# A hybrid encoder step on one core: the small group of the w_down product goes last, and the last pair of w_up runs its seven products in another order

## The chip, the cores and the metric

The kernel runs on one core of one Trainium2 chip. The metric is the device time of one execution in microseconds (us). Five engines work side by side: PE (TensorE, matrix products; PEld is its weight load), DVE (VectorE), ACT (ScalarE), POOL (GpSimd) and SP (SyncE, which here only issues transfers, in order, each after the waits that stand on it).

## The reference

One layer of a streaming encoder, for 512 prompt tokens and 128 sample tokens (640 in all), model width 2048. The part that the change touches is the channel mixer at the end:

```python
h = rmsnorm(x, g_pre_mlp) * (1 + scale_m) + shift_m
f = jnp.square(jax.nn.relu(h @ w_up)) @ w_down      # w_up 2048 x 8192, w_down 8192 x 2048
return x + gate_m * rmsnorm(f, g_post_mlp)
```

Before it stand the modulation, the input projection, two attentions, a linear recurrence and the output projection. All data is float32.

## The kernel before

**Products.** Every float32 operand is split into a rounded part and a rest (`split_into`, lines 85 and 86: a cast on ACT, a subtraction on DVE), and each product is three matmuls: high by high, high by rest, rest by high. Large products are taken as 2 x 2 blocks with seven block products in place of eight, after Strassen: sums and differences of blocks are formed on DVE, split, and multiplied; the results are added with signs.

**w_up.** The 8192 columns are 64 tiles of 128, taken in pairs j = 0 to 31. Three pairs are done plainly; pairs 3 to 31 are made by `up_pair(j)`, a generator with a `yield` after most of its products, so that the tail of one pair is interleaved with the head of the next. Its products run in the order 1, 2, 5, 6, 3, 7, 4, each 24 matmuls of 320 columns. Products 1, 2, 4 and 5 read the activations from the buffers `AH` and `AL` (mix_hi and mix_lo); products 3, 6 and 7 read sums of them from six tiles named X. Squared results go to DRAM in 16 blocks `u_dr[0]` to `u_dr[15]`; pair j writes into `u_dr[j // 2]`, so the last pair writes into `u_dr[15]`.

**w_down.** The stage after it adds up, into the tile `acc` (640 tokens by 2048 columns), the products of the blocks u_dr with w_down. Blocks 0 to 14 go through `groups`: a big group takes two blocks, cut into two halves h; the one small group takes a single block, its two halves being the two sides of the 2 x 2 scheme, so that it has half as many matmuls. The small group is block 0 and stands first; then come seven big groups, blocks 1 to 14. Block 15 is done plainly at the end (`down_cols`).

Each group has two passes over the columns, `columns(g, 0, ...)` and `columns(g, 1, ...)`, each with the products 1, 2, 5, 6, 3, 7, 4. In the first and second and in the third and seventh, the sample tokens ride along in a bank named y. A product needs its weights (`w_half`: w11 comes into the pool `wl`, the others w21, w12, w22 and v21 into a ring of six tiles named raw), the weights' sums (line 1173), their split, and its activations, which `u_operands(g)` loads from u_dr, combines and splits into `AX_h` and `AX_l` (ud_hi, ud_lo in the trace): a11, a12, a22 less a21, and so on, and the sample's s0, s1 and their difference. There is one set of these; `columns(g, 1, building)` makes the set of the next group place by place, as soon as a product has read the old one. For group 0 the whole generator is run ahead of the first pass. `gather` adds a bank into `acc` (lines 1123 to 1127).

AX_h and AX_l lie where mix_hi and mix_lo lay (tags `AH`, `AL`), and everything in the pool `ph3` (acc, `at`, `ar`, `wl`) lies where the X tiles and the tiles of w_up's results lay. Before the change a new pool waits for all that lay in its memory.

**Order.** A scheduler puts each engine's instructions in one fixed order; the order of the program and `tc.high_priority` steer it. SP issues nearly all transfers and waits at each.

Of the kernel before, what the change touches and what calls it, by code (L numbers as in the profile page):

```python
# [39 lines left out]
def stream_step(ctx: ExitStack, tc: tile.TileContext, I, O):  # L40
# [951 lines left out]
    with tc.tile_pool(name="up", bufs=1) as pl:  # L992
        def piece(name):
            return pl.tile([P, H2], F32, tag="c", bufs=7, name=name)

        def up_pair(j):

            w = up_blocks(j, "11 21 12 22")
            b1 = bank("mm", f"u1_{j}")
            up_product(1, b1, w["11"], f"a{j}", True)  # L1000
            c = piece(f"c11_{j}")
            S.copy(c, b1[:, :H2])
            yield
# [12 lines left out]
            with tc.high_priority(200):  # L1016
                V.tensor_add(w["11"], w["11"], w["22"])
            up_product(6, b1, w["11"], f"d{j}", False)
            c = piece(f"c12_{j}")
            S.copy(c, b1[:, :H2])  # L1020
            yield
            up_product(3, b2, w["22"], f"e{j}", False)
            V.tensor_add(c, b2[:, :H2], c)
            up_out(c, 2 * j + 1, 0, ALU.min)
            yield
            with tc.high_priority(200):
                V.tensor_add(w["12"], w["12"], w["22"])
            up_product(7, b1, w["12"], f"f{j}", False)
            V.tensor_add(p5, b1[:, :H2], p5)  # L1029
            up_out(p5, 2 * j + 1, 1, ALU.min)  # L1030
            yield
            with tc.high_priority(200):
                V.tensor_add(w["11"], w["11"], w["21"])
            up_product(4, b1, w["11"], f"g{j}", False)
            c = piece(f"c21_{j}")
            S.activation(c, b1[:, :H2], AF.Relu)
            S.activation(c, c, AF.Square)
            nc.sync.dma_start(u_dr[j // 2][:, 2 * j % 4, H2:], c)


        before = None
        for j in range(NPLAIN, 32):
            pair = up_pair(j)
            for i in range(5):
                next(pair)
                if before and i < 2:
                    next(before, None)
            before = pair
        for _ in before:
            pass  # L1050
# [4 lines left out]

    with tc.tile_pool(name="ph3", bufs=1) as pl:
        acc = pl.tile([P, NT, D], F32, name="acc")
        NBLK = 16  # L1060
        ORDER = (1, 2, 5, 6, 3, 7, 4)
        AX_h = act.tile([P, 8704], F32R, tag="AH", name="ud_hi")
        AX_l = act.tile([P, 8704], F32R, tag="AL", name="ud_lo")

        groups = [[((0, 0), (0, 1))]] + [[((n, h), (n + 1, h)) for h in range(2)] for n in range(1, NBLK - 1, 2)]

        def place(i, h):

# [3 lines left out]

        def u_part(g, r, t0, w, tag, name):

            x = pl.tile([P, len(groups[g]), 2, w], F32, tag=tag, bufs=1 if tag == "at" else 2, name=name)
            if len(groups[g]) == 2:
                nc.sync.dma_start(x.rearrange("p h k q -> p (h k) q"), u_dr[groups[g][0][r][0]][:, :, t0 : t0 + w])
            else:
                n, h = groups[g][0][r]
                nc.sync.dma_start(x[:, 0], u_dr[n][:, 2 * h : 2 * h + 2, t0 : t0 + w])  # L1080
            return x.rearrange("p h k q -> p (h k q)")

        def u_split(g, i, x):
            c = slice(place(i, 0).start, place(i, 0).start + x.shape[-1])
            split_into(AX_h[:, c], AX_l[:, c], x)

        def u_operands(g):

            one = lambda r, t, name: u_part(g, r, 256 * t, 256, "ar", f"{name}_{g}")
            u_split(g, 1, one(0, 0, "a11"))  # L1090
            yield
            u_split(g, 2, one(1, 0, "a12"))
            yield
# [11 lines left out]
            a = one(0, 0, "c11")  # L1105
            V.tensor_sub(a, a, one(0, 1, "c21"))
            u_split(g, 7, a)
            x1, x2 = [u_part(g, r, TP, TS, "ar", f"s{r}_{g}") for r in range(2)]
            u_split(g, -1, x1)
            u_split(g, -2, x2)  # L1110
            V.tensor_sub(x2, x2, x1)
            u_split(g, -3, x2)
            yield
            u_split(g, 4, one(1, 1, "b22"))
            yield
# [14 lines left out]
        def w_half(g, h, r, cb, tag, name):  # L1130

            n, q = groups[g][h][r]
            src = I["w_down"][n, cb][:, 1024 * q : 1024 * q + 1024]
            with tc.high_priority(200):
                if tag == "raw":
                    return load(src, f"{name}_{g}{cb}{h}")
                w = pl.tile([P, 1024], F32, tag=tag, bufs=4, name=f"{name}_{g}{cb}{h}")
                nc.sync.dma_start(w, src)
                return w
# [22 lines left out]
                        xs = [x[:, at + P * kk : at + P * kk + P] for x in (AX_h, AX_l)]  # L1162
                        dot(ps, xs, hi, lo, kk, s_first and h == 0 and kk == 0, s_last and h == nh - 1 and kk == 1)

        def columns(g, cb, building):

            nm, hs = f"d{g}{cb}", range(len(groups[g]))
            done = lambda: next(building, None)

            def more(a, b):  # L1170
# [6 lines left out]
            y1 = bank("md", f"{nm}y1")  # L1177
            w11 = [w_half(g, h, 0, cb, "wl", "w11") for h in hs]
            w21 = [w_half(g, h, 1, cb, "raw", "w21") for h in hs]
            product(g, 1, w11, b1, True, nm, (-1, y1, True, False))  # L1180
            for p in range(2):
                gather(p, cb, b1[p], 1)
            done()
            w12 = [w_half(g, h, 0, cb + 2, "raw", "w12") for h in hs]
            w22 = [w_half(g, h, 1, cb + 2, "raw", "w22") for h in hs]
            product(g, 2, w21, b3, True, nm, (-2, y1, False, True))
            for p in range(2):
                gather(p, cb, b3[p], 1)
# [1 line left out]
            done()  # L1190
            b2 = [bank("s", f"{nm}2{p}") for p in range(2)]
            more(w11, w12)
            product(g, 5, w11, b2, True, nm)
            for p in range(2):
                gather(2 + p, cb + 2, b2[p], -1)
            done()
            more(w11, w22)
            product(g, 6, w11, b1, False, nm)
            for p in range(2):
                gather(p, cb + 2, b1[p], -1)  # L1200
            done()
            y2 = bank("md", f"{nm}y2")
            product(g, 3, w22, b2, False, nm, (-3, y2, True, False))
            for p in range(2):
                gather(p, cb + 2, b2[p], -1)
            done()
            more(w12, w22)
            w21 = [w_half(g, h, 1, cb, "raw", "v21") for h in hs]
            product(g, 7, w12, b1, False, nm, (-1, y2, False, True))
            for p in range(2):  # L1210
                gather(2 + p, cb + 2, b1[p], -1)
            gather(4, cb + 2, y2, 1)
            done()
            more(w11, w21)
            product(g, 4, w11, b1, False, nm)
            for p in range(2):
                gather(2 + p, cb, b1[p], 1)
            done()

        for _ in u_operands(0):  # L1220
            pass
        for g in range(len(groups)):
            columns(g, 0, iter(()))
            columns(g, 1, u_operands(g + 1) if g + 1 < len(groups) else iter(()))


        n = NBLK - 1
# [168 lines left out]
```

## Time and profile before

| | us |
|---|---|
| three runs | 2752.97, 2754.78, 2750.55; median 2752.97 |
| the profiled execution | 2754.47 |
| its span | 2752.4 |
| PE busy in the span | 2651.9 (96%) |
| DVE busy | 1749.0 (64%) |
| ACT busy | 1075.0 (39%) |

The profiled execution's own time is 2.1 us above its span and 1.5 us above the median of the runs. PE is the engine that is nearly always busy; where it isn't, the profile says what it waited for.

### The profile page before, as it was taken

The numbers are of one execution on the slowest core, as the hardware profiler recorded it, in microseconds if no ns is written. First come the engines' busy times: TensorE is split into PE (matmuls) and PEld (weight loads), VectorE is DVE, ScalarE is ACT, GpSimd is POOL, SyncE is SP. The second block draws the span as 40 slices with busy tenths as digits, with TensorE's granted clock in tenths as the row PEclk, the third lists the DMA queues.
The fourth block names the chain that finished last, engine by engine and source line by source line (L and its number), as shares of the span: only waits on it lengthen the run. The fifth ranks groups of instructions, "written<-read, shape, count | busy, mean of one in ns | idle before, by whom it ended". The sixth has DMA issues, their size and how long they took to land.

```text
span 2752.4 us, 39345 instructions
## 1 busy us (share of the span) xinstructions
PE 2651.9 (96%) x15574; PEld 2271.7 (83%) x15574; DVE 1749.0 (64%) x2604; ACT 1075.0 (39%) x1641; POOL 53.2 (2%) x103
## 2 busy tenths in 40 slices
PE   7999999999999998999999999997799999999998
PEld 4677788778768777899999999996588887787886
DVE  4465534344354256766666666665888988888977
ACT  4264433334343256533333333332333433333432
POOL 0000000000000001100000000000000000000000
PEclk9999999999999999999999999999899999999999
DMA  8954565666665467733333333334444554554434
GB/s 324 358 161 149 154 193 173 218 209 193 217 218 168 138 218 262 241 114 119 105 118 111 111 118 107 116 113 148 148 155 152 161 173 141 158 179 131 155 106 171
DMA packets 189671, 461.29 MB, mean 168 GB/s; under 512 B 22920, under 2 KB 94248, under 8 KB 186928
## 3 DMA queue, kind: packets, MB, share of 16 engines
q1 hardware_dynamic: 185216, 441.68, 48.9%
q0 software_dynamic: 4128, 17.04, 1.7%
q8 instruction: 122, 2.00, 0.3%
q14 instruction: 61, 0.50, 0.1%
q10 hardware_dynamic: 144, 0.07, 0.0%
HBM read 411.33 MB, written 47.40 MB: 167 GB/s over the span
## 4 chain that ended last, share of the span: by engine, by line
PE 80%; DVE 10%; DMA 6%; issue 2%; ACT 2%; SPq 0%; POOL 0%; DVEq 0%; ACTq 0%; POOLq 0%
PE u L895 9%; PE u L896 9%; PE u L897 9%; PE d L1143 4%; PE d L1144 4%; PE d L1145 4%; PE wo L757 3%; PE wo L758 2%; PE wo L759 2%; DVE d_l L86 2%; DVE ud_lo L86 2%; DMA c<-u_dr 2%; PE mm_ps L142 2%; DVE acc L1123 1%; DMA u<-in_w_up_dram 1%
## 5 line engine op out<-in xcount | busy, mean ns | idle before, releaser
L85 ACT CAST d_h<-w 128x1024 fp32r<-128x1024 f32 x210 | 220.7, 1052 | 404.3 <-PE d L1145 112.8
L1143 PE MATMUL d<-d_h,ud_hi 128*128 128x512 f32 x840 | 330.8, 394 | 23.7 <-ACT ud_hi L85 10.2
L1144 PE MATMUL d<-d_l,ud_hi 128*128 128x512 f32 x840 | 330.0, 393 | 2.8 <-DVE d_l L86 2.8
L1145 PE MATMUL d<-d_h,ud_lo 128*128 128x512 f32 x840 | 328.6, 392 | 1.8 <-DVE ud_lo L86 1.8
L86 DVE TENSOR_TENSOR d_l<-w,d_h 128x1024 fp32r<-128x1024 f32 x210 | 255.5, 1222 | 92.3 <-ACT d_h L85 79.3
L1143 PEld LDWEIGHTS d<-d_h,ud_hi 128*128 128x128 f32 x840 | 158.7, 189 | 62.5 <-DVE acc L1123 14.1
L1144 PEld LDWEIGHTS d<-d_l,ud_hi 128*128 128x128 f32 x840 | 159.1, 189 | 36.9 <-DVE d_l L86 4.2
L1145 PEld LDWEIGHTS d<-d_h,ud_lo 128*128 128x128 f32 x840 | 159.1, 189 | 36.5 <-DVE ud_lo L86 3.5
L1123 DVE TENSOR_TENSOR acc<-acc,d 128x512 f32<-128x512 f32 x208 | 137.4, 682 | 7.7 <-PE d L1145 7.7
L758 PE MATMUL wo<-wo_l,mix_hi 128*128 128x512 f32 x320 | 125.8, 393 | 1.4 <-DVE wo_l L86 1.4
L757 PE MATMUL wo<-wo_h,mix_hi 128*128 128x512 f32 x320 | 126.5, 396 | 0.0
L759 PE MATMUL wo<-wo_h,mix_lo 128*128 128x512 f32 x320 | 125.5, 393 | 0.0
L86 DVE TENSOR_TENSOR wo_l<-wo_r,wo_h 128x1024 fp32r<-128x1024 f32 x48 | 58.6, 1224 | 101.4 <-ACT wo_h L85 98.6
L1173 DVE TENSOR_TENSOR w<-w,w 128x1024 f32<-128x1024 f32 x90 | 109.3, 1221 | 0.7
L86 DVE TENSOR_TENSOR a_l<-u,a_h 128x1024 fp32r<-128x1024 f32 x41 | 50.2, 1225 | 71.2 <-ACT a_h L85 71.2
L85 ACT CAST wo_h<-wo_r 128x1024 fp32r<-128x1024 f32 x48 | 50.1, 1050 | 108.9 <-PE wo L759 96.8
L86 DVE TENSOR_TENSOR g_l<-u,g_h 128x1024 fp32r<-128x1024 f32 x29 | 35.5, 1225 | 64.6 <-ACT g_h L85 64.6
L757 PEld LDWEIGHTS wo<-wo_h,mix_hi 128*128 128x128 f32 x320 | 60.5, 189 | 16.3 <-issue 3.5
L211 PE MATMUL zg<-h_hi,zg_h 128*128 128x320 f32 x224 | 74.0, 330 | 0.0
L211 PE MATMUL zx<-h_hi,zx_h 128*128 128x320 f32 x224 | 73.7, 329 | 0.0
L85 ACT CAST b_h<-u 128x1024 fp32r<-128x1024 f32 x41 | 43.0, 1048 | 75.5 <-PE u L896 60.1
L895 PE MATMUL u<-mix_hi,g_h 128*128 128x320 f32 x232 | 71.8, 310 | 0.6 <-DVE p L1029 0.6
(1867 smaller groups left out, 7390.3 us busy)
## 6 DMA issues: line engine op xcount, KB each, us to landing
u<-in_w_up_dram SPq DMA_DIRECT2D x140, 512.0 KB
w<-in_w_down_dram SPq DMA_DIRECT2D x120, 512.0 KB
ma<-in_w_mod_dram SPq DMA_DIRECT2D x64, 512.0 KB
mm<-in_w_mod_dram SPq DMA_DIRECT2D x64, 512.0 KB
g<-in_w_mod_dram SPq DMA_DIRECT2D x64, 512.0 KB
wo_r<-in_w_out_dram SPq DMA_DIRECT2D x48, 512.0 KB
v<-in_w_down_dram SPq DMA_DIRECT2D x30, 512.0 KB
a<-u_dr SPq DMA_DIRECT2D x28, 512.0 KB
```

Of the source, the lines that this page charges most:

```text
L85: S.copy(hi, raw)
L86: V.tensor_sub(lo, raw, hi.bitcast(F32))
L757: PE.matmul(ps, xh, wh, start=first, stop=False)
L758: PE.matmul(ps, xh, wl, start=False, stop=False)
L759: PE.matmul(ps, xl, wh, start=False, stop=last)
L895: PE.matmul(out, hi[:, c], xh[:, k, :], start=first and k == 0, stop=False, skip_group_check=True)
L896: PE.matmul(out, hi[:, c], xl[:, k, :], start=False, stop=False, skip_group_check=True)
L897: mm = PE.matmul(out, lo[:, c], xh[:, k, :], start=False, stop=k == 7, skip_group_check=True)
L1123: (V.tensor_add if sign > 0 else V.tensor_sub)(dst, dst, ps)
L1143: PE.matmul(ps, xs[0], hi[:, c], start=first, stop=False, skip_group_check=True)
L1144: PE.matmul(ps, xs[0], lo[:, c], start=False, stop=False, skip_group_check=True)
L1145: PE.matmul(ps, xs[1], hi[:, c], start=False, stop=last, skip_group_check=True)
```

## The change

The diff has four parts. The small group moves from the front (block 0) to the back (block 14), so the first big group is blocks 0 and 1. The last pair of w_up gets a function of its own, `last_pair`, with the products in the order 1, 5, 2, 3, 4, 6, 7 and without yields after the second. The pool ph3 is opened with `reuse_waits="tile"`, so that each of its tiles waits for what lay under it alone. And the operands of group 0 are no longer made ahead of its first pass but by a generator `own`, one step ahead of each product of that pass; of group 0 the tiles that others take from the pool `ar` come from the ring raw, which exists before ph3, and its sample operands are made first.

```diff
+        def last_pair(j):
+            w = up_blocks(j, "11 12 21 22")
+            b1, b2 = bank("mm", f"u1_{j}"), bank("s", f"u2_{j}")
+            up_product(1, b1, w["11"], f"a{j}", True)
...
+            V.tensor_add(w["11"], w["11"], w["12"])
+            up_product(5, b2, w["11"], f"c{j}", True)
...
+            yield
+            b3 = bank("ot"[j % 2], f"u3_{j}")
+            up_product(2, b3, w["21"], f"b{j}", True)
...
+            up_product(3, b2, w["22"], f"e{j}", False)
...
+            b4 = bank("ot"[1 - j % 2], f"u4_{j}")
+            up_product(4, b4, w["21"], f"g{j}", True)
...
+            up_product(6, b1, w["11"], f"d{j}", False)
+            V.tensor_add(c12, b1[:, :H2], c12)
+            up_out(c12, 2 * j + 1, 0, ALU.min)
+            V.tensor_add(w["12"], w["12"], w["22"])
+            up_product(7, b1, w["12"], f"f{j}", False)
+            V.tensor_add(p5, b1[:, :H2], p5)
+            up_out(p5, 2 * j + 1, 1, ALU.min)
+            V.tensor_add(c21, b1[:, :H2], c21)
+            up_out(c21, 2 * j, 1, ALU.max)
...
-            pair = up_pair(j)
+            pair = up_pair(j) if j < 31 else last_pair(j)
...
-    with tc.tile_pool(name="ph3", bufs=1) as pl:
+    with tc.tile_pool(name="ph3", bufs=1, reuse_waits="tile") as pl:
...
-        groups = [[((0, 0), (0, 1))]] + [[((n, h), (n + 1, h)) for h in range(2)] for n in range(1, NBLK - 1, 2)]
+        groups = [[((n, h), (n + 1, h)) for h in range(2)] for n in range(0, NBLK - 2, 2)] + [[((NBLK - 2, 0), (NBLK - 2, 1))]]
...
+            if g == 0 and tag == "ar":
+                x = raw_tile(shape, name)
+            else:
+                x = pl.tile(shape, F32, tag=tag, bufs=1 if tag == "at" else 2, name=name)
...
+            def of_sample():
+                x1, x2 = [u_part(g, r, TP, TS, "ar", f"s{r}_{g}") for r in range(2)]
+                u_split(g, -1, x1)
+                u_split(g, -2, x2)
+                V.tensor_sub(x2, x2, x1)
+                u_split(g, -3, x2)
             u_split(g, 1, one(0, 0, "a11"))
+            if g == 0:
+                of_sample()
             yield
...
-        def columns(g, cb, building):
+        def columns(g, cb, own, building):
             nm, hs = f"d{g}{cb}", range(len(groups[g]))
+            next(own, None)
...
+            next(own, None)
             product(g, 1, w11, b1, True, nm, (-1, y1, True, False))
...
-        for _ in u_operands(0):
-            pass
+        none = iter(())
+        own = u_operands(0)
         for g in range(len(groups)):
-            columns(g, 0, iter(()))
-            columns(g, 1, u_operands(g + 1) if g + 1 < len(groups) else iter(()))
+            columns(g, 0, own, none)
+            columns(g, 1, none, u_operands(g + 1) if g + 1 < len(groups) else none)
+            own = none
```

A `next(own, None)` like the one shown stands ahead of each of the seven products. The numbers of matmuls are the same: counted from the last one of w_up, the first matmul into the y bank is number 445 of the w_down stage in both programs, in the second pass of group 1 before and in the first pass of group 1 now.

SP's queue at the end of w_up, before. Names such as w11_000 read: which block of weights, group, columns, half; a11_0 is an operand of group 0; c12, p5 and c21 of 31 are the last pair's results on their way to u_dr[15].

```order
L72 DMA w21_010_17844<-in_w_down_dram 128x1024 [waits DMAHW0_49,DVE_49]
L72 DMA w12_030_17874<-in_w_down_dram 128x1024 [waits DMAHW1_49,DVE_49]
L903 DMA u_dr15_132<-c12_31_17510 128x320 [waits DMAHW2_49,DVE_49]
L903 DMA u_dr15_132<-p5_31_17479 128x320 [waits DMAHW3_49,DVE_49]
L1038 DMA u_dr15_132<-c21_31_17604 128x320 [waits DMAHW4_49,Activation_49]
L1138 DMA w11_000_17668<-in_w_down_dram 128x1024 [waits DMAHW4_49,DMAHW5_49,DMAHW3_49,DMAHW6_49,DMAHW2_49,PE_49]
L1138 DMA w11_010_17842<-in_w_down_dram 128x1024
L1080 DMA a11_0_17616<-u_dr0_117 128x2x256 [waits DMAHW7_49]
L1080 DMA a12_0_17620<-u_dr0_117 128x2x256 [waits DMAHW0_49]
```

The same queue with the change.

```order
L1117 DMA a12_0_17646<-u_dr1_118 128x4x256 [waits DMAHW1_49,DVE_49]
L72 DMA w12_020_17696<-in_w_down_dram 128x1024 [waits DMAHW2_49,DVE_49]
L72 DMA w12_021_17698<-in_w_down_dram 128x1024 [waits DMAHW3_49,DVE_49,Activation_49]
L72 DMA w22_020_17700<-in_w_down_dram 128x1024 [waits DMAHW4_49,DMAHW1_49,DVE_49]
L72 DMA w22_021_17702<-in_w_down_dram 128x1024 [waits DMAHW5_49,DVE_49]
L903 DMA u_dr15_132<-c12_31_17509 128x320 [waits DMAHW6_49]
L903 DMA u_dr15_132<-p5_31_17414 128x320 [waits DMAHW7_49,DVE_49]
L903 DMA u_dr15_132<-c21_31_17542 128x320 [waits DMAHW0_49,DVE_49]
L1185 DMA w11_000_17638<-in_w_down_dram 128x1024 [waits PE_49]
L1185 DMA w11_001_17640<-in_w_down_dram 128x1024 [waits DMAHW2_49]
L1117 DMA a22_0_17704<-u_dr1_118 128x4x256 [waits DMAHW3_49]
```

The operands a11, s0, s1 (further up) and a12 moved ahead of the last stores. The load of w11 no longer waits for a transfer to end, but it stands behind the three stores as before.

DVE at the end of w_up with the change (before, the rows from c12 to c21 are followed at once by the split of w11).

```order
L86 TENSOR_TENSOR ud_lo_17617<-a11_0_17618,ud_hi_17616 128x1024 [waits DMAHW0_49,PE_49,Activation_49]
L86 TENSOR_TENSOR ud_lo_17617<-s0_0_17622,ud_hi_17616 128x512 [waits DMAHW2_49,Activation_49]
L86 TENSOR_TENSOR ud_lo_17617<-s1_0_17624,ud_hi_17616 128x512 [waits DMAHW4_49,Activation_49]
L1067 TENSOR_TENSOR c12_31_17509<-u1_31_17321,c12_31_17509 128x320 [waits PE_49]
L1135 TENSOR_TENSOR s1_0_17624<-s1_0_17624,s0_0_17622 128x512 [waits DVE_49]
L902 SCALAR_TENSOR_TENSOR c12_31_17509<-c12_31_17509 128x320 [waits DVE_49]
L86 TENSOR_TENSOR ud_lo_17617<-a12_0_17646,ud_hi_17616 128x1024 [waits DMAHW1_49,Activation_49]
L86 TENSOR_TENSOR ud_lo_17617<-s1_0_17624,ud_hi_17616 128x512 [waits Activation_49]
L1071 TENSOR_TENSOR p5_31_17414<-u1_31_17321,p5_31_17414 128x320 [waits PE_49]
L1073 TENSOR_TENSOR c21_31_17542<-u1_31_17321,c21_31_17542 128x320 [waits DMAHW6_49]
L902 SCALAR_TENSOR_TENSOR p5_31_17414<-p5_31_17414 128x320 [waits DVE_49]
L902 SCALAR_TENSOR_TENSOR c21_31_17542<-c21_31_17542 128x320 [waits DVE_49]
```

What moved there: seven rows of the next stage's operands stand among the last pair's results, and c21 is now finished on DVE, last of the three, where ACT finished it before.

DVE between the small group and group 1, before: the last rows in which group 1's operands are made.

```order
L1098 SCALAR_TENSOR_TENSOR a22_1_17928<-a22_1_17928,b11_1_17954 128x1024 [waits DMAHW3_49,DVE_49]
L1173 TENSOR_TENSOR w12_121_18119<-w12_121_18119,w22_121_18123 128x1024 [waits DMAHW7_49]
L1102 SCALAR_TENSOR_TENSOR b12_1_17984<-a22_1_17928,b12_1_17984 128x1024 [waits DMAHW4_49,DVE_49]
L86 TENSOR_TENSOR ud_lo_17615<-a22_1_17928,ud_hi_17614 128x1024 [waits Activation_49]
L86 TENSOR_TENSOR ud_lo_17615<-b12_1_17984,ud_hi_17614 128x1024 [waits Activation_49]
L1106 TENSOR_TENSOR c11_1_18017<-c11_1_18017,c21_1_18019 128x1024 [waits DMAHW7_49,DMAHW5_49]
L86 TENSOR_TENSOR ud_lo_17615<-c11_1_18017,ud_hi_17614 128x1024 [waits Activation_49]
```

The same operands of group 1 with the change, made in the second pass of the big group 0.

```order
L1148 SCALAR_TENSOR_TENSOR a22_1_18149<-a22_1_18149,b11_1_18192 128x1024 [waits DMAHW4_49,DVE_49]
L1152 SCALAR_TENSOR_TENSOR b12_1_18244<-a22_1_18149,b12_1_18244 128x1024 [waits DMAHW5_49,DVE_49]
L86 TENSOR_TENSOR d0171_l_18278<-w12_031_18054,d0171_h_18277 128x1024 [waits Activation_49]
L1170 TENSOR_TENSOR acc_17615<-acc_17615,d0120_18111 128x512 [waits PE_49]
L1170 TENSOR_TENSOR acc_17615<-acc_17615,d0121_18112 128x512 [waits PE_49]
L86 TENSOR_TENSOR ud_lo_17617<-a22_1_18149,ud_hi_17616 128x1024 [waits Activation_49]
L86 TENSOR_TENSOR d0140_l_18323<-w11_010_17994,d0140_h_18322 128x1024 [waits Activation_49]
L86 TENSOR_TENSOR ud_lo_17617<-b12_1_18244,ud_hi_17616 128x1024 [waits DVE_49]
```

Before, they stand in a row of their own; now splits and gathers of group 0's products 7, 3 and 4 stand between them.

## Rows read from the trace of the kernel before

**Rows 1.** The page: busy us per engine; PE's busy tenths in 40 slices.
```profile
PE 2651.9 (96%) x15574; PEld 2271.7 (83%) x15574; DVE 1749.0 (64%) x2604; ACT 1075.0 (39%) x1641; POOL 53.2 (2%) x103
...
PE   7999999999999998999999999997799999999998
```

**Rows 2.** Waits of PE from 1880 to 2000 us: total us, times, longest.
```profile
PE d10y L1143 <- ACT ud_hi L85: 16.7, 1, 16.7
PE d L1143 <- ACT ud_hi L85: 10.2, 1, 10.2
```

**Rows 3.** Chain of waits around 1887 us, in order of time: start, us, what.
```profile
1886.62 0.16 PE u L897
1886.80 0.45 ACT c L1036
1887.27 0.48 ACT c L1037
1887.77 1.76 DMA u_dr<-c
1889.71 0.33 SPq L1138
...
1890.58 0.42 SPq L1080
1891.04 5.51 DMA a<-u_dr
```

**Rows 4.** Timeline of ACT: start, us, engine, line, operation.
```profile
1894.37 1.99 ACT L85 CAST d_h<-w 128x1024 fp32r<-128x1024 f32 x2 [6.63 <-DMA w<-in_w_down_dram]
```

**Rows 5.** Timeline of SP and DVE in the second wait.
```profile
1975.94 0.52 SPq L1077 DMA_DIRECT2D c<-u_dr  x1
1982.24 2.85 SPq L1077 DMA_DIRECT2D s<-u_dr  x2
...
1974.69 1.23 DVE L86 TENSOR_TENSOR ud_lo<-b,ud_hi 128x1024 fp32r<-128x1024 f32 x1
1980.99 1.23 DVE L1106 TENSOR_TENSOR c<-c,c 128x1024 f32<-128x1024 f32 x1 [5.07 <-DMA c<-u_dr]
```

**Rows 6.** First and last start of y-bank matmuls: d11y is group 1, second pass.
```profile
L1143 PE MATMUL d11y<-d_h,ud_hi x16: 389/389/390, 2031.8 to 2071.9; 128*128 128x512 f32 x16
L1143 PE MATMUL d21y<-d_h,ud_hi x16: 388/389/390, 2131.5 to 2171.6; 128*128 128x512 f32 x16
L1143 PE MATMUL d30y<-d_h,ud_hi x16: 388/389/393, 2182.4 to 2222.6; 128*128 128x512 f32 x16
L1143 PE MATMUL d70y<-d_h,ud_hi x16: 388/389/390, 2585.9 to 2626.0; 128*128 128x512 f32 x16
L1143 PE MATMUL d71y<-d_h,ud_hi x16: 389/389/397, 2635.0 to 2675.1; 128*128 128x512 f32 x16
```

**Rows 7.** Stretches: length, busy PE, PEld, DVE, ACT, POOL, granted clock, DMA share, GB/s.
```profile
1888.00:1897.00 9.00, 0.07 (x1) 0.07 (x1) 1.55 (x2) 2.55 (x4) 0.00 (x0) 0.67 0.75 239
1986.00:1992.00 6.00, 5.93 (x18) 4.66 (x19) 3.90 (x5) 3.16 (x5) 0.00 (x0) 0.66 0.24 56
2140.00:2240.00 100.00, 98.32 (x434) 80.82 (x433) 85.51 (x92) 38.01 (x38) 0.00 (x0) 1.00 0.50 157
```

**Rows 8.** Timeline at the end of w_up: the last result on DVE, its store.
```profile
1882.44 0.49 DVE L1029 TENSOR_TENSOR p<-u,p 128x320 f32<-128x320 f32 x1 [2.44 <-PE u L897]
1882.96 0.49 DVE L902 SCALAR_TENSOR_TENSOR p<-p 128x320 f32<-128x320 f32 x1
...
1883.48 0.33 SPq L903 DMA_DIRECT2D u_dr<-p  x1
```

**Rows 9.** Chain of waits later on: two splits, then two gathers, back to back.
```profile
2054.30 2.27 DVE d_l L86 x2
...
2063.56 1.20 DVE acc L1123 x2
```

**Rows 10.** Waits of PE from 2550 us to the end.
```profile
PE dn L1143 <- DVE acc L1240: 1.5, 1, 1.5
PE d L1143 <- DVE acc L1123: 0.6, 1, 0.6
```

More of the change, by code (lines that the diff above doesn't have):

```diff
@@ L1038, in up_pair @@
             nc.sync.dma_start(u_dr[j // 2][:, 2 * j % 4, H2:], c)
+        def last_pair(j):
+            w = up_blocks(j, "11 12 21 22")
+            b1, b2 = bank("mm", f"u1_{j}"), bank("s", f"u2_{j}")
+            up_product(1, b1, w["11"], f"a{j}", True)
+            c11 = piece(f"c11_{j}")
+            S.copy(c11, b1[:, :H2])
+            yield
+            V.tensor_add(w["11"], w["11"], w["12"])
+            up_product(5, b2, w["11"], f"c{j}", True)
+            p5 = piece(f"p5_{j}")
+            S.copy(p5, b2[:, :H2])
+            yield
+            b3 = bank("ot"[j % 2], f"u3_{j}")
+            up_product(2, b3, w["21"], f"b{j}", True)
+            V.tensor_add(c11, b3[:, :H2], c11)
+            up_out(c11, 2 * j, 0, ALU.max)
+            up_product(3, b2, w["22"], f"e{j}", False)
+            c12 = piece(f"c12_{j}")
+            S.copy(c12, b2[:, :H2])
+            V.tensor_add(w["11"], w["11"], w["22"])
+            V.tensor_add(w["21"], w["21"], w["11"])
+            b4 = bank("ot"[1 - j % 2], f"u4_{j}")
+            up_product(4, b4, w["21"], f"g{j}", True)
+            c21 = piece(f"c21_{j}")
+            S.copy(c21, b4[:, :H2])
+            up_product(6, b1, w["11"], f"d{j}", False)
[7 more added lines that the diff above has]
+            up_out(c21, 2 * j, 1, ALU.max)
         before = None
         for j in range(NPLAIN, 32):
-            pair = up_pair(j)
+            pair = up_pair(j) if j < 31 else last_pair(j)
             for i in range(5):
-                next(pair)
+                next(pair, None)
                 if before and i < 2:
@@ L1073, in u_part @@
         def u_part(g, r, t0, w, tag, name):
-            x = pl.tile([P, len(groups[g]), 2, w], F32, tag=tag, bufs=1 if tag == "at" else 2, name=name)
+            shape = [P, len(groups[g]), 2, w]
+            if g == 0 and tag == "ar":
+                x = raw_tile(shape, name)
+            else:
+                x = pl.tile(shape, F32, tag=tag, bufs=1 if tag == "at" else 2, name=name)
             if len(groups[g]) == 2:
@@ L1107, in u_operands @@
             u_split(g, 7, a)
[L1108 to L1112, printed above, removed]
+            if g:
+                of_sample()
             yield
@@ L1185, in columns @@
             w22 = [w_half(g, h, 1, cb + 2, "raw", "w22") for h in hs]
+            next(own, None)
             product(g, 2, w21, b3, True, nm, (-2, y1, False, True))
@@ L1192, in columns @@
             more(w11, w12)
+            next(own, None)
             product(g, 5, w11, b2, True, nm)
@@ L1197, in columns @@
             more(w11, w22)
+            next(own, None)
             product(g, 6, w11, b1, False, nm)
@@ L1202, in columns @@
             y2 = bank("md", f"{nm}y2")
+            next(own, None)
             product(g, 3, w22, b2, False, nm, (-3, y2, True, False))
@@ L1208, in columns @@
             w21 = [w_half(g, h, 1, cb, "raw", "v21") for h in hs]
+            next(own, None)
             product(g, 7, w12, b1, False, nm, (-1, y2, False, True))
@@ L1214, in columns @@
             more(w11, w21)
+            next(own, None)
             product(g, 4, w11, b1, False, nm)
```

## The prediction

> **What bounds the kernel now.** I read the page first: PE is busy 96% of the span, and its slices are full except at the start and in two slices marked 7 and 7 behind the middle [rows 1]. A slice is 68.8 us, so those two run from about 1858 to 1995 us, and that is where w_up ends and w_down begins. So PE is the bound, and a change can only win what PE loses there, or lose elsewhere. The list of PE's waits in that stretch has two large entries, both on the cast of an operand into ud_hi: 10.2 us ahead of the small group's first product and 16.7 us ahead of the sample part of group 1 [rows 2].
>
> The chain of waits explains the first. w_up's last matmul ends at 1886.62 + 0.16 = 1886.78 us, which I call E. ACT finishes c21, its store travels 1.76 us, only then does SP issue the first load of w11, and behind it a11, which lands 5.51 us after its issue [rows 3]. The whole pool waited for the last store. The second wait is a chain of loads and DVE steps: c21 of group 1 is issued at 1975.94, DVE idles 5.07 us for it, the sample operands are issued only at 1982.24 [rows 5]. They stand so late because a small group has half as many matmuls in which to hide the making of a big group's operands.
>
> How much PE loses in all I take from markers, not from single gaps. The y bank's first matmul of group 1's second pass starts at 2031.8 us [rows 6], 145.0 us after E, and is the 445th of w_down. One undisturbed pass of 216 matmuls takes 2635.0 - 2585.9 = 49.1 us [rows 6], or 0.2273 us each, so 444 of them are 100.9 us. **Lost before: 44.1 us.** Two waits make 26.9 of it; the remaining 17.2 are small waits while the operands of the small group drip in, and half clock: after the second wait 18 matmuls took 5.93 us at a granted clock of 0.66 where 4.09 would do [rows 7], so 1.8 us, and likewise after the first.
>
> With the change the same 445th matmul belongs to the first pass of group 1. From there on both programs have equal matmuls and six passes each in which a next group is built. So the sum is: 44.1 less what the new program loses up to that marker, less what the small group costs at its new place.
>
> **Part 1, the start.** The last pair's order frees AH and AL after product 4, two products or 2 x 24 matmuls before E, and a11, the sample operands and a12 are split in that time; on DVE they stand ahead of p5 and c21. These two, with their squares, are four operations of 320 columns after E. One follows the next in 0.52 us or less [rows 8], so c21's last starts at about E + 1.5. Its store is issued 0.52 us later [rows 8], at E + 2.0, and then the first load of w11 at E + 2.4: SP is in order, and that load stands behind the three stores although its own memory (where X tiles for product 3 lay) has long been free. Before it was E + 2.9. From the issue of w11 to its cast took 1894.37 - 1889.71 = 4.66 us [rows 3, 4], so now the cast starts at E + 7.1, the first matmul can go at E + 8.1 (two casts took 1.99 us [rows 4]), and the third needs the rest from DVE 1.14 us later [rows 9]. I take 9.0 us lost, and 1.9 for the half clock after the pause. The operands are there by then, so the wait that was 10.2 us shrinks little. Bounds: 7 us if the load lands like a lone one, 12 if the blocks of w22, issued just ahead of it, hold it up: two blocks of 512 KB at the 239 GB/s of the stretch after E [rows 7] are 4.4 us, of which about two lie before its issue.
>
> The Trainium skill (DMA: Bandwidth & Descriptors, "Anatomy of one DMA") puts a load at 2.0 us plus its bytes at 436 GB/s, which is 3.2 us for 512 KB; the row has 4.66, with three loads close behind. By the page the sum would end 1.5 us lower; I stay with the row.
>
> **Part 2, group 0's own operands.** They are now made inside its first pass. DVE's work there: 14 splits and 8 sums of weights at 1.14 us [rows 9], 16 gathers at 0.60 [rows 9], and of the operands 11 large steps at 1.14 and four small ones at 0.60. That is 25.0 + 9.6 + 14.9 = 49.5 us, less the 4.7 us that are done before E: 44.8 us for a pass of 49.1 on PE. The order is tight. Followed step by step from E + 9.2, the operands of products 3 and 7 are ready within a microsecond of PE's reaching them: those of 5 and 6 have some 5 and 1.5 us to spare, since a21, b11, b12, c11 and c21 each take a place in the ring when a weight or an operand is split, and four of its six places hold w12 and w22. A late load of 1 or 2 us is thus paid in part. Price between 0 and the 13.5 us that remain of the 17.2 without the two clock losses, which is what the same drip cost the small group. It is nearer to the low end, since a product has twice the matmuls to cover a load; I take 2.
>
> **Part 3, the second pass of group 0** builds group 1, as in every later group: such a pass took 2182.4 - 2131.5 = 50.9 us against 49.1 [rows 6], so 1.8 us.
>
> **Part 4, the small group at the end.** Its operands are made in a big pass, at half their size, so the 16.7 us are gone and have no heir: block 15 follows, whose parts need no seven products. In the group itself DVE has 14 splits, 8 sums, 32 gathers, block 15's five activation tiles at 0.6 and its two first splits and the last small operands: 25.0 + 19.2 + 3.0 + 2.3 + 1.0 = 50.5 us against 49.1 of PE. So DVE is the bound by 1.4 us; I take 1.5, with bounds 0 and 6 (a wait of about 0.6 for a gather [rows 10] at ten places, as products are short). The end is the same as before, with its wait of 1.5 us on a gather [rows 10]; late weights still wait for the last product.
>
> At nothing I cost the new order within the last pair: nine products of pairs 30 and 31 interleave as before, each with its weights loaded earlier; c12's sum now stands behind two small splits on DVE, up to 1 us if they are late. Bytes and matmuls are unchanged, and at a DMA share of 0.50 in the steady stage [rows 7] the loads there have room.
>
> **Sum.** Lost after: 9.0 + 1.9 + 2.0 + 1.8 + 1.5 = 16.2 us. Won: 44.1 - 16.2 = 27.9. The profiled execution took 2754.47, so 2726.6; the median of the runs shown, 2752.97, is 1.5 lower, which makes **2725 us**.
>
> **Rivals.**
>
> *Group 0's operands drip as before.* For it: the margins of a microsecond in part 2, and DVE at 85.51 of 100 us already in the steady stage [rows 7]. Against: products twice as long. Loss 10.9 + 13.5 + 1.8 + 1.5 = 27.7, a win of 16.4: 2736.5 us.
>
> *All of it hides.* Start at the low bound 7, parts 2 and 4 at nothing: loss 7 + 1.9 + 1.8, a win of 33.4: 2719.5 us. For it: a11 no longer loads with w11.
>
> *The ring locks the loads in turn: slower.* Eight loads of group 0's first pass (a21, b11, b12, c11, c21, two v21, b22) pass through the two places that w12 and w22 leave. If each had to wait for the split before it, a trip is 5.51 us of load [rows 3] plus 1.14 of DVE: 6.6, eight times 53 us, of which PE's own work would cover some 15. Loss 11 + 38 + 3 = 52, time 2761. It decides when PE waits for each load by more than 27.9 / 8 = 3.5 us. Against: places are given to whoever needs one when any is free, and c11, c21 need theirs only 25 us after the start.
>
> *The change frees nothing.* w11 behind the stores and late operands of group 0 keep the first wait, and the build of group 1 meets the same wait in pass two. The 16.7 us came from a build of a big group in a pass of 24.5 us; in one of 49.1 such builds cost 1.8 [rows 6]. 2750 us.
>
> **Chances.** Forecast (2720 to 2731): 0.60. All hides or better, below 2720: 0.12. Drip, 2731 to 2742: 0.18. Nothing: 0.03. Slower: 0.07. The range 2718 to 2737 leaves out the slow case, the null case and about half of the tails, in all 2 in 10. Less than 0.2%, 5.5 us, can't be told from no change here. Faster by more: 0.90; same 0.03; slower 0.07.
>
> **What would show it.** After the change the first matmul of w_down should start some 8 us after the last of w_up, with casts of ud_hi (a11, s0, s1, a12) before E on ACT; the y bank of group 1's first pass should start 100.9 + 14.7 = 116 us after E; no wait of PE beyond 3 us in between, and none on ud_hi ahead of group 1. The small group should take 49 to 52 us late in the kernel. I am wrong on part 1 if w11 is issued before c21's store or lands later than 6 us; on part 2 if PE waits on ud_lo or ud_hi in products 5, 6, 3 or 7 for more than 2 us in sum; on part 4 if PE's waits on acc add up to more than 6 us in the last 120 us.

## The result, and the profile after

The changed kernel takes 2718.48 us in the median of 4 runs (2715.2 to 2722.79), the kernel before beside it 2753.26 (2750.55 to 2754.78): a ratio of 0.9876, with a 95% interval of 0.9859 to 0.9893. Forecast were 2725 us within 2718 to 2737. The profiled execution took 2722.79 us with a span of 2720.8, against 2754.47 and 2752.4, so the two traces to be compared are 31.6 us apart.

The page after (busy us by engine; PE's busy tenths) has lost the two slices of 7 [rows 1]; one 8 is left in their place:

```profile
PE 2644.4 (97%) x15574; PEld 2268.9 (83%) x15574; DVE 1748.6 (64%) x2606; ACT 1073.8 (39%) x1640; POOL 53.2 (2%) x103
...
PE   7999999999999999899999999998999999999998
```

PE's waits from 1860 to 2110 us after (total us, times, longest), to be laid beside [rows 2]; the 1.6 us lie behind 2100 us:

```profile
PE d L1190 <- ACT d_h L85: 10.2, 1, 10.2
PE d L1190 <- DVE acc L1172: 2.5, 1, 2.5
PE d L1190 <- DVE acc L1170: 1.6, 1, 1.6
PE u L895 <- DVE c L1067: 0.9, 1, 0.9
```

The second wait, 16.7 us, is gone. The first has the same length to a tenth of a microsecond, but another cause: before it was for the operand (ud_hi), now it is for the weights of the first product (d_h). The chain of waits after (start, us, what), in the place of [rows 3], says why:

```profile
1887.11 0.16 PE u L897
1887.29 0.49 DVE p L1071
1887.79 0.40 DVE c L1073
1888.18 0.41 DVE p L902
1888.61 0.33 SPq L903
1889.03 0.60 SPq L903
1889.69 6.61 DMA w<-in_w_down_dram
1896.32 1.05 ACT d_h L85
1897.41 1.22 PE d L1190 x2
```

w_up's last matmul ends at 1887.26 us (E). The load of w11 goes behind two stores at E + 2.43, and takes 6.61 us to its cast. The operands were ready: ACT had cast a11 at 1879.45 us. (The rows of DVE's order shown with the change hold six steps of these operands, not seven.)

The y-bank markers after (line, count, ns, first and last start), with d10y as the 445th matmul in the place of d11y [rows 6]:

```profile
L1190 PE MATMUL d00y<-d_h,ud_hi x16: 389/389/390, 1902.5 to 1943.0; 128*128 128x512 f32 x16
L1190 PE MATMUL d01y<-d_h,ud_hi x16: 388/389/396, 1952.1 to 1992.2; 128*128 128x512 f32 x16
L1190 PE MATMUL d10y<-d_h,ud_hi x16: 388/389/390, 2003.9 to 2044.0; 128*128 128x512 f32 x16
```

The marker comes 2003.9 - 1887.26 = 116.6 us after E, against 145.0 before: 28.4 us won up to there. Windows after (us, busy PE, PEld, DVE, ACT, POOL, granted clock, DMA share, GB/s): the wait, the start behind it, two stretches of the first pass, and the small group.

```profile
1887.26:1897.41 10.15, 0.00 (x0) 0.00 (x0) 1.71 (x5) 1.04 (x1) 0.00 (x0) 0.71 0.93 319
1897.41:1907.00 9.59, 9.55 (x32) 7.30 (x33) 9.56 (x9) 3.04 (x3) 0.00 (x0) 0.77 0.78 266
1907.00:1917.00 10.00, 10.00 (x45) 8.26 (x44) 9.80 (x11) 4.76 (x5) 0.00 (x0) 1.00 0.53 152
1927.00:1937.00 10.00, 10.00 (x46) 8.18 (x45) 9.60 (x11) 3.41 (x4) 0.00 (x0) 1.00 0.93 309
```
```profile
2600.00:2625.00 25.00, 25.00 (x111) 20.45 (x110) 24.47 (x31) 9.44 (x12) 0.00 (x0) 1.00 0.27 85
2625.00:2650.00 25.00, 25.00 (x112) 20.73 (x111) 23.73 (x31) 8.11 (x9) 0.00 (x0) 1.00 0.42 136
```

From the marker on, the trace after is 2720.8 - 2003.9 = 716.9 us long, the one before 720.6. These 3.7 us I don't count as the change's (see the last section).

### The profile page after: what moved, and what is told of

Same layout as the page of the kernel before. It is cut to its first block, busy times and chain, and to the rows that moved or that the text cites. A ratio compares the mean times of both kernels' runs of the same rounds, so it can differ in the third digit from the quotient of the medians.

```text
span 2720.8 us, 39339 instructions
## 1 busy us (share of the span) xinstructions
PE 2644.4 (97%) x15574; PEld 2268.9 (83%) x15574; DVE 1748.6 (64%) x2606; ACT 1073.8 (39%) x1640; POOL 53.2 (2%) x103
## 4 chain that ended last, share of the span: by engine, by line
PE 81%; DVE 9%; DMA 5%; issue 3%; ACT 1%; POOL 0%; SPq 0%; DVEq 0%; POOLq 0%; ACTq 0%
PE u L895 9%; PE u L896 9%; PE u L897 9%; PE d L1190 5%; PE d L1191 4%; PE d L1192 4%; PE wo L757 2%; PE wo L758 2%; PE wo L759 2%; DVE d_l L86 2%; PE mm_ps L142 2%; DVE ud_lo L86 1%; PE g_ps L142 1%; PE zx L211 1%; DMA c<-u_dr 1%
## 5 line engine op out<-in xcount | busy, mean ns | idle before, releaser
L1190 PE MATMUL d<-d_h,ud_hi 128*128 128x512 f32 x840 | 329.9, 393 | 20.8 <-ACT d_h L85 10.2
L1190 PEld LDWEIGHTS d<-d_h,ud_hi 128*128 128x128 f32 x840 | 158.4, 189 | 58.3 <-DVE acc L1170 12.2
L895 PE MATMUL u<-X,f_h 128*128 128x320 f32 x232 | 71.8, 310 | 0.9 <-DVE c L1067 0.9
```

The costliest lines, as they stand in the source:

```text
L895: PE.matmul(out, hi[:, c], xh[:, k, :], start=first and k == 0, stop=False, skip_group_check=True)
L1190: PE.matmul(ps, xs[0], hi[:, c], start=first, stop=False, skip_group_check=True)
```

## The experiments

Theory at the outset: the group order takes the second wait, and the last pair, the piecewise release and group 0's own operands take the rest of the loss. Rivals: the group order alone, or the other edits alone, do it all. Twelve kernels were run. Execution times scatter by several us, so beside the time each row has the length of the stretch itself: E to the 445th matmul of w_down, in the profiled execution (100.9 us without a loss). The kernels ran in several sets, each beside the kernel before; its medians there were 2753.17, 2756.51 and 2753.58 us. So kernels are better compared by their ratios than by their medians. From "changed, operands all ahead" down, the intervals overlap with that of the changed kernel: there only the markers, of one execution each, tell the kernels apart.

| kernel | median us | ratio to before (95%) | E to marker, us |
|---|---|---|---|
| before | 2753.26 | 1 | 145.0 |
| group order alone | 2744.27 | 0.9970 (0.9954-0.9986) | 139.6 |
| all but group order | 2747.65 | 0.9972 (0.9957-0.9987) | 138.6 |
| samples' place alone | 2739.54 | 0.9953 (0.9937-0.9970) | 135.5 |
| group order and samples' place | 2727.95 | 0.9898 (0.9882-0.9913) | 127.4 |
| changed, operands all ahead | 2725.74 | 0.9889 (0.9874-0.9905) | 123.0 |
| changed, whole pool waits | 2723.54 | 0.9893 (0.9869-0.9918) | 119.3 |
| changed, product 2 first | 2721.92 | 0.9882 (0.9864-0.9901) | 118.8 |
| changed, POOL loads w11, a21 and b11 in pool | 2724.44 | 0.9904 (0.9882-0.9925) | 118.3 |
| changed | 2718.48 | 0.9876 (0.9859-0.9893) | 116.6 |
| changed, run again | 2719.97 | 0.9889 (0.9865-0.9912) | 115.8 |
| changed, POOL loads w11 | 2714.23 | 0.9850 (0.9834-0.9866) | 114.3 |
| changed, old pair order | 2716.50 | 0.9872 (0.9850-0.9894) | 114.1 |
| changed, old pair order, POOL loads w11 | 2716.68 | 0.9858 (0.9840-0.9876) | 113.2 |

**Group order alone.** In the kernel before:

```diff
-groups = [[((0, 0), (0, 1))]] + [... for n in range(1, NBLK - 1, 2)]
+groups = [... for n in range(0, NBLK - 2, 2)] + [[((NBLK - 2, 0), (NBLK - 2, 1))]]
```

> The kernel before with one line changed: the small group goes last; the last pair, the whole-pool wait and group 0's operands made all ahead stay as they were. Theory (the parts add up: the group order takes the second wait of 16.7 us, the other edits take the small waits while group 0's operands come in): the second wait is gone, the first of about 10 us stays, and the small waits behind it stay, some 13 us of them; 2730 to 2740 us. Rival (the group order is the whole gain, the other edits are worth nothing): 2716 to 2722 us, as the changed kernel.

Neither: 2744.27 us. Its waits of PE, and SP's and DVE's timeline ahead of the larger:

```profile
PE d00y L1143 <- ACT ud_hi L85: 16.2, 1, 16.2
PE d L1143 <- ACT ud_hi L85: 11.5, 1, 11.5
```
```profile
1916.74 0.52 SPq L1077 DMA_DIRECT2D c<-u_dr  x1
1922.66 2.85 SPq L1077 DMA_DIRECT2D s<-u_dr  x2
...
1921.40 1.23 DVE L1106 TENSOR_TENSOR c<-c,c 128x1024 f32<-128x1024 f32 x1 [4.69 <-DMA c<-u_dr]
```

This is [rows 5] over again, one group earlier: the wait went from group 1's sample part to group 0's. The samples stand last in a chain of operands, behind c21, and the first product needs them. Group 1's samples stand there too, but its operands are now made in a full pass, and no wait on ud_hi stands ahead of d10y. Group 0's are made with no pass before them. So two things go together here: samples that come last, and too little work of PE to cover the chain.

**All but the group order.** The changed kernel with the line above undone.

> The changed kernel with the small group put back to the front, all other edits kept. Theory: in the second pass of the small group the operands of a big group are built in 25 us of PE work again, so PE waits there for 12 to 20 us; the start is about as in the changed kernel; 2732 to 2746 us. Rival (the second wait came from the whole-pool wait or the operands made ahead, not from the group order): below 2725 us.

2747.65 us, just above the theory's range; the second wait is back:

```profile
PE d10y L1190 <- ACT ud_hi L85: 15.8, 1, 15.8
```

Alone, each half of the change is worth 0.3%; together they are worth 1.2%. Each half leaves one wait of 16 us: the group order alone leaves that ahead of d00y, the other edits alone leave that ahead of d10y.

**Samples' place and group order.** The kernel before with the group order and, for group 0 alone, the samples made early:

```diff
 u_split(g, 1, one(0, 0, "a11"))
+if g == 0:
+    of_sample()
...
-x1, x2 = [u_part(g, r, TP, TS, "ar", f"s{r}_{g}") for r in range(2)]
...
+if g:
+    of_sample()
```

> The kernel before with the small group last and, of the other edits, one alone: group 0's sample operands are made behind a11 and not behind c21. Two buffers for the operands, all of them ahead of the first pass, the whole-pool wait and the last pair as before. Theory A (place of the samples): the wait of 16.2 us ahead of d00y, seen with the group order alone, is gone; later operands still come one behind the other through two buffers and cost some us each; 2728 to 2738 us. Theory B (the two buffers or the spreading are what counts): the same loss shows up at products 5 to 7 in place of the sample part; 2740 to 2747 us.

2727.95 us, theory A: the large wait is gone, and small ones remain:

```profile
PE d L1149 <- ACT ud_hi L85: 11.6, 1, 11.6
PE d L1151 <- DVE ud_lo L86: 6.3, 2, 3.4
```

With one more edit than the group order alone, it takes 12.2 of the 23.0 us by which that kernel stood behind the changed one at the marker (139.6 - 116.6). The other 10.8 belong to the rest of the edits; two of these are undone one by one below, and the place of group 0's operands in the ring was not tried alone.

**Samples' place alone.** The kernel before with the five sample lines moved up behind a11 for every group. This changes a part of the computation: in a group's second pass the sample part reads operands that already are those of the next group. Its operations and bytes are the same, but the sample matmuls of a second pass now wait for the next group's operands.

> The kernel before, small group first, with one edit: in every group the sample operands are made behind a11 and not behind c21. Theory A (the second wait, 16.7 us, came from the samples' place behind c21 in the chain of operands): the wait ahead of d10y is gone or below 4 us; what is left of it shows as small waits in products 5 to 7 of group 1; 2735 to 2745 us. Theory B (it came from the short pass, in which a big group's operands can't be made in time wherever the samples stand): waits of 12 us or more in sum fall to group 1's other operands; 2746 to 2753 us.

2739.54 us, theory A, with the small group still first: the marker comes 9.5 us sooner, no wait stands ahead of d10y, and the largest left is the first:

```profile
PE d L1143 <- ACT ud_hi L85: 14.2, 4, 10.1
PE d01y L1143 <- ACT ud_hi L85: 3.6, 1, 3.6
```

The 3.6 us ahead of d01y are such a wait that the edit itself brings in. It is no way to build the kernel, but it shows that with the samples early even the short pass leaves no second wait. So the wait needs both, the late samples and the short pass.

**Group 0's operands all ahead again.** In the changed kernel:

```diff
-own = u_operands(0)
+for _ in u_operands(0):
+    pass
+own = none
```

> The changed kernel with group 0's operands written all ahead of its first pass again, as before; their order (samples behind a11), their place in the ring, the group order, the last pair and the pool's piecewise release stay. Theory A (the wait of 16 us of the sample part goes because the samples stand ahead of c11 and c21 and have slots of the ring, not because the operands are spread over the pass): no wait on a sample, PE's waits up to the marker within 5 us of the changed kernel's; 2716 to 2725 us. Theory B (spreading the operands over the pass is what hides them): weights stand behind operands in the ring, PE waits for 10 us or more beyond the first wait; 2729 us or more.

2725.74 us, just above theory A's range: no wait on ud_hi for a sample and 16.9 us of waits in all up to the marker against 12.7, as theory A has it, but 6.4 us more at the marker. SP shows that now a weight of the ring stands ahead of w11 (E is 1881.96 us here):

```profile
1883.73 0.38 SPq L903 DMA_DIRECT2D u_dr<-c  x1
1886.67 0.34 SPq L72 DMA_DIRECT2D w<-in_w_down_dram  x1
1887.11 0.85 SPq L1185 DMA_DIRECT2D w<-in_w_down_dram  x2
```

**The whole pool waits again.** `reuse_waits="tile"` taken out of the changed kernel.

> The changed kernel with the next stage's pool waiting as a whole again, as before; all other edits stay. Theory: the first load of w11 now waits for the last store to land, which took 1.76 us, and not only behind its issue, so the first wait grows from 10.2 to 11.5 to 12.5 us and nothing else changes; 2718 to 2723 us. Rival (the piecewise release is what the start rests on): the first wait grows by 4 us or more, 2722 us or more.

The first wait is 13.5 us, 3.3 more, and the marker comes 2.7 later: between theory and rival, with the median of 2723.54 on the rival's side. So by the marker the piecewise release is worth some 3 us; by the ratios (0.9893, and 0.9889 for the changed kernel in the same set) the two can't be told apart. The store that w11 waits for took longer to land than the 1.76 us of [rows 3]: SP is free at 1889.38 us and w11 goes at 1894.90.

```profile
1888.68 0.70 SPq L903 DMA_DIRECT2D u_dr<-c  x1
1894.90 0.81 SPq L1185 DMA_DIRECT2D w<-in_w_down_dram  x2
```

**The old order of the last pair.** In the changed kernel:

```diff
-pair = up_pair(j) if j < 31 else last_pair(j)
+pair = up_pair(j)
```

> The changed kernel with the last pair of w_up in the order of all pairs; AH and AL are then free only with the last matmul of w_up, and the casts of a11 and the samples come after it. Theory (the first product waits for the load of w11, which stands behind the last store either way and is cast 6 to 7 us after its issue): the casts of the operands fit into that time, first wait 9 to 12 us, 2717 to 2724 us, no difference beyond 4 us. Rival (the freed memory is what lets w_down begin early): the first wait grows by the 4 to 5 us of the operands' casts and subtractions, 2723 us or more.

2716.5 us, just below the theory's range, and as it has it: no loss. E is 1885.44 us here, and ACT's timeline shows the operands cast behind E and still ahead of w11:

```profile
1885.81 1.04 ACT L85 CAST ud_hi<-a 128x1024 fp32r<-128x1024 f32 x1
1887.12 1.12 ACT L85 CAST ud_hi<-s 128x512 fp32r<-128x512 f32 x2
1893.40 1.04 ACT L85 CAST d_h<-w 128x1024 fp32r<-128x1024 f32 x1 [1.70 <-DMA w<-in_w_down_dram]
```

w11 was issued at 1888.56 us here with one weight close ahead of it, and its cast came 4.84 us later. The first wait is 9.1 us. So last_pair releases memory that nobody is waiting for, as long as w11 comes late.

**Product 2 ahead of product 1 in the first pass** (its weights come through the ring and lie there before E).

```diff
-product(g, 1, w11, b1, True, nm, (-1, y1, True, False))
...
+if g == 0 and cb == 0:
+    two(True)
```

> The changed kernel with product 2 ahead of product 1 in the very first pass of w_down; the sample part's first and last flags move with it, and the sums are the same but for their order. The weights of product 2 go to the ring and were loaded before the last matmul of w_up, and a12 is split before it. Theory (the first wait of 10.2 us is for the load of w11, nothing else): the first matmul of w_down starts within 4 us of the last of w_up, the load of w11 passes under product 2's 36 matmuls (8 us), 6 to 8 us won: 2711 to 2714 us. Rival (something else, DVE's splits or free split buffers, ends the wait just as late, or w11 is late again by as much behind product 2): 2717 us or more.

2721.92 us, the rival. PE starts at once, at E + 0.07, as the theory has it, but it then waits 4.1 us for w11 behind product 2 and 6.1 us for product 5's operand:

```profile
PE d L1190 <- ACT ud_hi L85: 6.4, 2, 6.1
PE d L1190 <- ACT d_h L85: 4.1, 1, 4.1
```

**w11's first two loads issued by POOL**, with the old pair order and then in the changed kernel:

```diff
-nc.sync.dma_start(w, src)
+(nc.gpsimd if (g, cb) == (0, 0) else nc.sync).dma_start(w, src)
```

> The changed kernel with the last pair in the order of all pairs, and the two loads of w11 of the first pass issued by POOL in place of SP, so that no store stands ahead of them. Theory (the first wait is for w11, and its memory is freed by a product that is not the last when the pair's order is the old one): the loads go 2 to 4 us before the end of w_up, the first wait falls from 9.1 to 3 to 6 us; 2709 to 2714 us. Rival (the memory is freed by the last matmul, or a load issued by POOL lands as late as one behind the stores): first wait 7 us or more, 2715 us or more.

> The changed kernel with the two loads of w11 of the first pass issued by POOL. Here the last product of the last pair reads the tiles that lie where w11 goes, so the load can't start before the last matmul of w_up. Theory: only the 2.4 us behind the stores are won and something of the two that the load took longer behind the blocks of w22, first wait 6 to 9 us, 2714 to 2719 us. Rival (the load is free earlier and only SP's order held it): as with the old pair's order and POOL, 2709 to 2714 us.

With the old pair order the first wait falls to 7.3 us only, the rival's number but not for its reasons: POOL issues the loads at 1877.80 us, 7.6 us before E (1885.38 here), and w11's cast now stands on ACT behind the sample casts, which stand behind E. In the changed kernel my expectation on the memory was wrong. POOL issues the loads at 1872.46 us, 11.4 us before E (1883.86 here): the memory was long free, as part 1 of the prediction had it, and only SP's order had held them. ACT casts w11 before E, and the wait of 10.2 us is gone; the largest is 2.4 us, for DVE's split:

```profile
1872.46 1.08 POOL L1185 DMA_DIRECT2D w<-in_w_down_dram  x2 [720.12 <-PE u L897]
```
```profile
PE d L1191 <- DVE d_l L86: 3.5, 3, 2.4
PE d L1192 <- DVE ud_lo L86: 3.1, 3, 1.4
```

Yet the marker gains 1.5 to 2.3 us and not 8. The waits for splits in the lines above take their place, and DVE's timeline shows the largest stop: a sum for product 5 whose load is late, with later splits of weights behind it in DVE's fixed order:

```profile
1887.89 2.35 DVE L86 TENSOR_TENSOR d_l<-w,d_h 128x1024 fp32r<-128x1024 f32 x2
...
1902.43 1.22 DVE L1145 TENSOR_TENSOR a<-a,a 128x1024 f32<-128x1024 f32 x1 [6.44 <-DMA a<-u_dr]
```

**The same with a21 and b11 in the pool's own buffers**, so that they need no place in the ring:

```diff
-if g == 0 and tag == "ar":
+if g == 0 and tag == "ar" and name not in ("a21_0", "b11_0"):
```

> The changed kernel with w11's two loads of the first pass issued by POOL, and two of group 0's operands, a21 and b11, in the pool's own two buffers and not in the ring. With POOL's loads alone the first wait of 10 us went, but only 2 to 3 us were won by the marker, since DVE then stood 6.4 us waiting for a21, whose load had no place in the ring. Theory (the start's loss has moved to that load): a21 is issued 3 us earlier or more, DVE's wait for it falls below 3 us, the marker comes 109 to 112 us after the end of w_up, 2 to 5 us less than with POOL's loads alone; 2708 to 2713 us. Rival (the loads of the start share a DMA that is already busy nine tenths of the time, so that one earlier makes another late): 113 to 116 us, 2713 to 2718 us.

118.3 us and 2724.44: the theory falls, and it is worse than the rival. DVE's wait grew to 9.73 us, but not because a21 came later. SP's issues of a22 and a21 took from 1891.25 to 1897.11, and 4.6 us of SP's waits there are for the last stores to land, much as the 4.8 us with POOL's loads alone. Counted from E (1888.29 here, 1883.86 there), DVE starts the sum with a21 at E + 12.7, against E + 18.6.

```profile
1891.25 5.86 SPq L1117 DMA_DIRECT2D a<-u_dr  x2
```
```profile
1890.02 1.22 DVE L86 TENSOR_TENSOR d_l<-w,d_h 128x1024 fp32r<-128x1024 f32 x1
1900.97 1.22 DVE L1145 TENSOR_TENSOR a<-a,a 128x1024 f32<-128x1024 f32 x1 [9.73 <-DMA a<-u_dr]
1902.11 2.35 DVE L86 TENSOR_TENSOR d_l<-w,d_h 128x1024 fp32r<-128x1024 f32 x2
```
```profile
PE d L1191 <- DVE d_l L86: 8.7, 2, 6.3
```

What changed is DVE's order: the sum now stands ahead of two splits of weights that stood well ahead of it with POOL's loads alone. So DVE idles for a21 while PE waits 6.3 us for a split whose cast was done at 1890.01 us. This kernel therefore doesn't tell what an earlier a21 is worth with DVE's order kept.

**The changed kernel again**, for this set.

> The changed kernel as it is, once more, so that the other kernels of this set stand against it on the same chip: 2715 to 2723 us, marker 115 to 118 us after the end of w_up.

2719.97 us and 115.8: the marker repeats within 0.8 us.

## Why the prediction was right

The mechanism of the sum held up to the marker. Of the 29.4 us that it had there (44.1 - 14.7), 28.4 came, with some 1.5 us too little for the start with its half clock, 1.5 too much for group 0's operands and 0.9 too little for the pass that builds group 1; that the first two cancel is luck. The loss after is 116.6 - 100.9 = 15.7 us, by its parts:

- **Start.** w11 was issued at E + 2.43, forecast was 2.4, and the operands were cast before E. Mis-sized is the load: 6.63 us from issue to cast in place of 4.66, so the first matmul came at E + 10.15 and not at 8.1. That is beyond the 6 us which the prediction had named as its sign of being wrong on part 1: the path was right, the size was not. The upper bound had named blocks of w22 issued just ahead: four blocks of w12 and w22 went from 1881.78 us on, for 4.67 us, and the window of the wait has a DMA share of 0.93 at 319 GB/s, where [rows 7] have 0.75 and 239. The 4.84 us with one block ahead (old pair order) points the same way; blocks alone were not varied. The Trainium skill (DMA: Bandwidth & Descriptors, "Anatomy of one DMA") gives 3.2 us for such a size, an estimate from its figures, which it has for a DMA issued by GpSimd; the prediction had left that limit out. The three rows here, by SP and up to a cast, lie above it, and so do the loads issued by POOL, in pairs and beside others: 5.6, 6.1 and 6.4 us to landing in the three kernels that have them. No run here has such a load by itself.
- **Half clock.** 32 matmuls took 9.59 us at a mean granted clock of 0.77; at 0.2273 us each they are 7.3. So 2.3 us, forecast 1.9 and 0.9 for DVE's split (the latter inside the 9.0). The clock alone covers nearly all of it (9.59 x 0.77 = 7.4); what the split cost beside it can't be told apart.
- **Group 0's own operands.** d01y starts 49.6 us after d00y, 0.5 more than an undisturbed pass; forecast 2. PE is full in that pass.
- **The pass that builds group 1.** 2003.9 - 1952.1 = 51.8, so 2.7 us; forecast 1.8. The row is the 2.5 us on acc.
- **Small group at the end.** PE is busy 50.00 of 50.00 us, with DVE at 48.2: nothing lost, forecast 1.5.

The step that failed without hurting the number is the reason for the second wait: "They stand so late because a small group has half as many matmuls in which to hide the making of a big group's operands." That is half of it. The samples' place alone removed the wait with the small group still first, and later groups with the samples in the old place but a full pass show no wait on ud_hi: it takes both. The group order alone brought the wait back ahead of group 0, whose operands have no pass to hide in. So what part 4 booked to the group order needs the samples' early place as well. Likewise the last pair, at which part 1 begins, is not shown to be worth anything: with its order undone the kernel was no slower, and the marker came 1.7 to 2.5 us sooner.

Behind the marker 3.7 us were won where I had 1.5 lost. Of the 5.2 between them, 1.5 are the small group's, which cost nothing, and 1.5 a wait on acc that the pass building a small group doesn't have (waits on acc behind the marker: 9.6 us in 6 before, 8.1 in 5 after). The other 2.2 are inside what equal code shows (below).

The medians are 34.8 us apart, where the sum had 27.9. Up to the marker 1.0 less came than forecast, and E came 0.5 later; the surplus is the 5.2 behind it and 3 us by which the profiled executions lie closer together (31.6) than the medians. So 2718.48 us is only 0.5 above the low end of the range, and in the class below 2720 that had a chance of 0.12, though its story of a start at 7 us did not come true. That the number fell inside the range is in part luck.

Left open: a kernel better than both. POOL's loads of w11 in the changed kernel gave 2714.23 us, the lowest median, but their interval overlaps the changed kernel's, the marker shows only 1.5 to 2.3 us, and its profiled execution also had the shortest time behind the marker. Whether the 6.44 us of DVE can be had by issuing a22 and a21 ahead of the stores was not tried. In that kernel SP waits 4.8 us for those stores at another load of operands, which stands ahead of a21 in its queue.

## What to carry to other kernels

A wait of the same length before and after can be two different waits: read what ended it, not its size. When a long wait is removed, ask what stands last in the chain of loads that a product needs first; here it was the samples, and the wait showed wherever they came last and too little work covered the chain. Two halves of the change that each left such a wait for one group were worth 0.3% alone and 1.2% together. Memory released early is worth something only if the load that wants it isn't in a queue behind a store, and the next late load isn't just behind it. A kernel with a buffer moved can also get another order on an engine: compare the order before the cause is put down to the load.

## What the runs showed that I had not expected

Stretches with the same program differ between executions by more than most of these edits. E lay between 1882.0 and 1888.3 us over the kernels here, and in the eleven that end with the small group the time from the marker to the end lay between 713.8 and 720.8 us. The difference is the granted clock. In seven windows of 100 us from the marker on it is 0.99, 0.98, 1.00, 0.98, 0.98, 1.00 and 1.00 in the kernel whose tail took 720.8, and 1.00 in all seven in the one with 713.8; what is missing from 1.00 adds up to 7 us. PE was busy for 97.9 us or more of each; why the clock fell the runs don't show. The second window of each kernel:

```profile
2106.60:2206.60 100.00, 99.49 (x431) 81.65 (x430) 84.03 (x90) 37.81 (x38) 0.00 (x0) 0.98 0.49 156
```
```profile
2098.20:2198.20 100.00, 98.63 (x435) 81.16 (x434) 85.86 (x92) 38.08 (x38) 0.00 (x0) 1.00 0.50 158
```

So an edit of one stage is better judged by a marker in that stage, which came within 0.8 us in the one kernel that was profiled twice, than by one execution's span.
